# FFN GEMMs of a decoder step in Strassen's scheme: seven block products for eight, by token halves

## The chip, the cores and the metric

The kernel runs on one core of one Trainium2 chip. The metric is device time in microseconds of one launch; lower is better. A profiled execution of the same program gives the trace. All matmuls of interest are float32r: a float32 operand is split exactly into a high and a low float32r part, and one product is made of three matmuls (high by high, high by low, low by high).

## The reference, cut to what matters

One layer of a hybrid decoder on 1088 tokens (1024 prompt tokens and 64 sample tokens) of width 1024: a mixer of sliding-window attention and mLSTM heads, a memory cross-attention, then a SwiGLU FFN with 2816 hidden features, each behind an RMS norm, and a final RMS norm. The change is about the FFN:

```python
def swiglu(xn, w_gate, w_up, w_down):
    g = jnp.einsum('btd,df->btf', xn, w_gate)
    u = jnp.einsum('btd,df->btf', xn, w_up)
    return jnp.einsum('btf,fd->btd', jax.nn.silu(g) * u, w_down)
...
yp = yp + swiglu(rmsnorm(yp, g_ffn[l]), w_gate[l], w_up[l], w_down[l])
y_prompt = rmsnorm(yp, g_final)
```

All outputs, attention caches and mLSTM states among them, are unchanged by the change.

## The kernel before, in words

Activations lie feature-major: eight tiles of 128 features by 1088 tokens. A GEMM takes a weight tile of 128 by 128 as the stationary operand and streams tokens, in three chunks of 384, 384 and 320 columns (`CH`); `mm3` (L133 of the code before) issues the three matmuls of a split product and `gemm_chunk` sums them over the contraction tiles in one PSUM bank. `load_w` (L111) brings a weight tile by one DMA on SP's queue into `wraw`, ScalarE copies it to the high part `whi` (L102) and VectorE subtracts to the low part `wlo` (L103); each of the three has two buffers.

The stages follow one another: the input projection (x arrives, tile by tile, on SP's queue; token-major products `tok_gemm` for v, gates and mv; feature-major products for mq and mk), gates, memory keys, mLSTM in eight blocks of 128 tokens, attention with the output projection as filler, cross-attention by chunks, its output projection `co` with the operands of the FFN's norm (`nx.add` splits y times the norm weights into `nhi` and `nlo`; the norm's factor is applied to the product), and the FFN. In an mLSTM block, GpSimd makes the decay argument (`bc`, L503) and the weighted queries (`wb`, L586); the block's products wait for them.

The FFN runs over 22 hidden tiles in groups of two or four. For each tile: gate product (three chunks of 24 matmuls), the norm's factor on VectorE (L1002), Silu on ScalarE (L1004), the factor again on GpSimd (L1005), the up product, their product `h` (L1008) and its split into `hhi`, `hlo`. After each group the down product of the group is added to y in SBUF (L1018). The last group goes by token chunks of 416, 416 and 256 (`CHE`) with the final norm and the output behind it (L1025, L1032, L1043). FFN weights are read once.

The code is written in a framework that plans the order itself: it records the instructions with their dependences, simulates the engines with costs, and gives each engine the ready instruction that stands first in the code. So an instruction without inputs can stand on its engine far ahead of its place in the code. Each engine then executes in that fixed order, and a waiting instruction holds all behind it on its engine. On-chip buffers come from pools; an instruction that writes a reused buffer waits for its last readers.

Of the kernel before, what the change touches and what calls it, by code (L numbers as in the profile page):

```python
# [9 lines left out]
F32 = mybir.dt.float32  # L10
# [13 lines left out]
CHE = [(0, 416), (416, 832), (832, 1088)]   # where the last one ends the kernel  # L24
FT = 22                     # feature tiles of the FFN
GROUPS = [(0, 2), (2, 6), (6, 10), (10, 14), (14, 18), (18, 22)]
# [3 lines left out]
# columns of the vectors packed by the host  # L30
# [3 lines left out]
# columns of the constants  # L34
C_ID, C_ONE, C_CAUS, C_CAUSS, C_BM, C_M0, C_M1 = 0, 128, 256, 384, 448, 456, 712
C_N = 968
# columns of the constants for the gates
# [5 lines left out]
def tile_hymba_step(  # L43
    ctx: ExitStack,
    tc: tile.TileContext,
    xT, memT, win_f, win_a, win_b, wout, wcq, wck, wcv, wco, wg, wu, wd,
# [6 lines left out]
    cp = ctx.enter_context(tc.tile_pool(name="cp", bufs=1))  # L53
    wp = ctx.enter_context(tc.tile_pool(name="wp", bufs=2))
    sl = ctx.enter_context(tc.tile_pool(name="sl", bufs=1))
    tp = ctx.enter_context(tc.tile_pool(name="tp", bufs=10))
    sm = ctx.enter_context(tc.tile_pool(name="sm", bufs=4))
    dr = ctx.enter_context(tc.tile_pool(name="dr", bufs=1, space=bass.MemoryType.DRAM))
    ps = ctx.enter_context(tc.tile_pool(name="ps", bufs=1, space=bass.MemoryType.PSUM))

    BUFS = {"x": 16, "q": 4, "m": 4, "c": 9, "r": 2}

    def slot(tag, shape, dt=F32, name="slot"):
        return sl.tile([P] + shape, dt, tag=tag, name=name, bufs=BUFS[tag])

# [18 lines left out]
    def mm(out, lhsT, rhs, start=True, stop=True):  # L84
        return TE.matmul(out, lhsT, rhs, start=start, stop=stop)  # L85

# [1 line left out]
    c = cp.tile([P, C_N], F32, name="c")  # L88
    vv = cp.tile([P, V_N], F32, name="vv")
    nc.sync.dma_start(vv, vec)  # L90
    ident = c[:, C_ID:C_ID + P]
    ones = c[:, C_ONE:C_ONE + P]
    epsb = cp.tile([P, 1], F32, name="epsb")
# [29 lines left out]
    def load_ahead(srcs):  # L123
        """The weights in the order of their use, each loaded one step ahead of it."""
        todo, ahead = iter(srcs), []

        def step():
            for src, eng in todo:
                ahead.append(load_w(src, 8, eng=eng))
                break  # L130

        def next_w():
            step()  # L133
            return ahead.pop(0)

        step()
        return next_w

    def mm3(out, ahi, alo, bhi, blo, start, stop):
        mm(out, ahi, bhi, start, False)  # L140
        mm(out, ahi, blo, False, False)
        return mm(out, alo, bhi, False, stop)
# [14 lines left out]
    # ================= stage 1: x, split; sums of squares =================  # L157
    nc.scalar.preload_act_table_set("natural_log_exp_and_others")
    xs, xr = [], []
    for k in range(NK):  # L160
        xr.append(slot("cm"[k % 2], [T], name="xraw"))
        nc.sync.dma_start(xr[k], xT[k])
        hi, lo = slot("x", [T], F32R, name="xhi"), slot("x", [T], F32R, name="xlo")
# [16 lines left out]
    # the first two tiles run along with the arrival of x  # L180
# [24 lines left out]
    # token-major rstd  # L205
# [54 lines left out]
    for b in range(NB + 1):  # L260
        acc, m = tok_gemm(wb, b, 384)
# [94 lines left out]
    # rows (block, head) of prompt; rows (head) of sample  # L356
# [40 lines left out]
    # the weight of the state before the block, as rows  # L397
# [33 lines left out]
    # the upper half of the partitions holds the odd heads  # L431
# [10 lines left out]
    for i, (wi_, pre) in ((1, (2, 0.125)), (2, (3, None)), (3, (4, None))):  # L442
# [3 lines left out]
        for c0, c1 in CH:  # L446
            acc = gemm_chunk(w, xs, c0, c1)
# [4 lines left out]
    # M4: mq pair 0, mq pair 1, mk pair 0, mk pair 1; later the head outputs  # L452
# [4 lines left out]
    # the heads' norm weights with the half of sigmoid(x) = (1 + tanh(x / 2)) / 2  # L457
# [5 lines left out]
    def mlstm_ps():  # L463
        """PSUM for num | den of the heads: the row tiles of odd and even heads go to different banks."""
# [3 lines left out]
    def mlstm_w(src, m):  # L468
        """The weight of the state, by head pair, on the partitions of the heads."""
# [6 lines left out]
    def mlstm_head_out(nb, blk, m, c0, junk):  # L476
        """num | den of the heads in PSUM -> normalised heads, transposed into M4."""
# [22 lines left out]
    def mlstm_S(blk, m, c0, bc, caus):  # L500
        """S^T[s, t] of the four heads, weighted."""
# [73 lines left out]
    for blk in range(NB):  # L575
        if blk == 4:
            mlstm_sample()
# [39 lines left out]
    def softmax_pieces(pieces, mx, nbias, es=None):  # L617
        """P = exp(0.125 s + bias) / (sum + es) in place for the (row, piece) scores."""
# [121 lines left out]
    y = []  # L740

    def load_y():
        for k in range(NK):
            t = slot("mx"[k // 4], [T], name="y")
# [3 lines left out]
    class Next:  # L748
        """Operands of the GEMM behind a norm: (y * g) split; rstd goes on its output."""
# [86 lines left out]
    # weights of this stage in the order of their use  # L836
# [31 lines left out]
    def cross_unit(pair, f):  # L868
        """Two blocks of prompt tokens, one pair of heads."""
# [110 lines left out]
    nx = Next(V_FFN, tags="xxxxxxqq")  # L980
    for ci, (c0, c1) in enumerate(CH):
        for d in range(NK):
            co(d, c0, c1)
            nx.add(d, c0, c1, V if d > 3 else G)
            if ci and d == 1:
                nx.finish([CH[ci - 1]])

# [1 line left out]
    fin = Next(V_FIN, parts=False)  # L989
    for gi, (f0, f1) in enumerate(GROUPS):  # L990
        hs = []
        for f in range(f0, f1):
            wg_, wu_ = load_w(wg[f], NK), load_w(wu[f], NK)
            hi, lo = slot("c", [T], F32R, name="hhi"), slot("c", [T], F32R, name="hlo")
            for c0, c1 in CH:
                n = c1 - c0
                ga = gemm_chunk(wg_, nx.xs, c0, c1)
                if f + c0 == 0:
                    nx.finish([CH[-1]])
                    fr = nx.rstd  # L1000
                t = tmp([384], name="gate")[:, :n]
                V.tensor_tensor(t, ga, fr[:, c0:c1], ALU.mult)  # L1002
                with tc.issue_after(nx.done.ins) if f < 2 else nullcontext():
                    A.activation(t, t, AF.Silu)  # L1004
                G.tensor_tensor(t, t, fr[:, c0:c1], ALU.mult)  # L1005
                ua = gemm_chunk(wu_, nx.xs, c0, c1)
                h = tmp([384], name="h")[:, :n]
                V.tensor_tensor(h, ua, t, ALU.mult)  # L1008
                split(hi[:, c0:c1], lo[:, c0:c1], h)
            hs.append((hi, lo))  # L1010
        nf = f1 - f0
        if gi < len(GROUPS) - 1:
            for d in range(NK):
                if d % 2 == 0:
                    w = load_w([wd[d + i, :, f0:f1, :] for i in range(2)], 2 * nf)
                for c0, c1 in CH:
                    acc = gemm_chunk(w, hs, c0, c1, (d % 2) * nf)
                    V.tensor_tensor(y[d][:, c0:c1], y[d][:, c0:c1], acc, ALU.add)  # L1018
    ws = [load_w([wd[2 * i + z, :, f0:f1, :] for z in range(2)], 2 * nf, tag="x" if i > 1 else None)
          for i in range(4)]  # L1020
    tc.keep_in_program_order(nc.scalar.preload_act_table_set("natural_log_exp_and_others"))

    def out(d, c0, c1):
        t = tmp([448], name="yo")[:, :c1 - c0]
        V.scalar_tensor_tensor(t, y[d][:, c0:c1], gcol(V_FIN, d), fin.rstd[:, c0:c1], ALU.mult, ALU.mult)  # L1025
        nc.sync.dma_start(o_y[d, :, c0:c1], t)

    for ci, (c0, c1) in enumerate(CHE):
        end = ci == len(CHE) - 1
        for d in range(NK):  # L1030
            acc = gemm_chunk(ws[d // 2], hs, c0, c1, (d % 2) * nf)
            V.tensor_tensor(y[d][:, c0:c1], y[d][:, c0:c1], acc, ALU.add)  # L1032
            fin.add(d, c0, c1, V if end and d > 4 else G, end and d == NK - 1)
            if end:
                A.activation(y[d][:, c0:c1], y[d][:, c0:c1], AF.Copy, scale=gcol(V_FIN, d))
            if ci:
                out(d, *CHE[ci - 1])
        fin.finish([(c0, c1)])
    c0, c1 = CHE[-1]
# [136 lines left out]
```

## Time and profile before

| what | value |
|---|---|
| time, median of 3 runs | 1384.12 us (1383.92 to 1391.01) |
| span of the profiled execution, first to last instruction | 1380.3 us |
| own time of the profiled execution | not given; the median is 3.8 us above the span |
| TensorE busy | 1343.5 us, 97% of the span |
| VectorE, ScalarE, GpSimd busy | 622.2, 444.6, 190.3 us |
| moved by DMA | 88.26 MB |

The page is read from the busy table to the slices and then to the chain of waits; the stage that changes is then taken out of the trace by windows. Matmuls are pipelined, so the duration of one (over 300 ns) is no rate: the distance from one start to the next is.

### The profile page before, as it was taken

To read this page: it belongs to the slowest core of one execution; us is meant where nothing else is said; L and a number is where in the kernel's file an instruction comes from. 1 tells how busy PE (TensorE), PEld (TensorE's weight loads), DVE (VectorE), ACT (ScalarE), POOL (GpSimd) and SP (SyncE) were. 2 spreads that over 40 slices of the span, in tenths; PEclk is the share of its full clock that TensorE was granted. 3 is DMA by queue.
4 is the path that set the end of the run, shared out by engine and by line. 5 is a ranking of instruction groups with operands and counts; after the bars stand their busy time and mean duration, and the time that the engine had idled before them with its cause. 6 is when DMAs were issued, how large, how long until landed. Compare 5 with 4: busy or idle time off the path is not lost.

```text
span 1380.3 us, 20544 instructions
## 1 busy us (share of the span) xinstructions
PE 1343.5 (97%) x8352; PEld 1266.2 (92%) x8352; DVE 622.2 (45%) x1373; ACT 444.6 (32%) x1024; POOL 190.3 (14%) x167
## 2 busy tenths in 40 slices
PE   7999999999999898999999999999999999999997
PEld 6999988887888786799999999999999999999997
DVE  7224345467766778835323332332233232423245
ACT  4322332447754666721221011201121121112133
POOL 3000110100003551110111011101110011001123
PEclk9999999999999999999999999999999999999999
DMA  5122413110311224102111111111112120111113
GB/s 228 40 74 62 146 56 121 38 47 16 131 46 57 97 92 163 52 16 62 47 31 62 46 47 31 51 42 46 47 32 61 31 62 31 62 32 50 43 37 124
DMA packets 38807, 88.26 MB, mean 64 GB/s; under 512 B 6593, under 2 KB 14209, under 8 KB 38713
## 3 DMA queue, kind: packets, MB, share of 16 engines
q1 hardware_dynamic: 38713, 86.95, 19.6%
q8 instruction: 66, 1.08, 0.3%
q14 instruction: 28, 0.23, 0.1%
HBM read 79.54 MB, written 7.38 MB: 63 GB/s over the span
## 4 chain that ended last, share of the span: by engine, by line
PE 58%; DVE 3%; ACT 1%; issue 0%; DMA 0%; POOL 0%; DVEq 0%; ACTq 0%; POOLq 0%
PE mm L85 57%; DVE nlo L109 1%; PE o L85 0%; DVE y L955 0%; PE pt L85 0%; DVE nb L866 0%; DVE wlo L103 0%; DMA ck<-cm_k 0%; PE sc L85 0%; ACT sp L887 0%; ACT sq L773 0%; DVE qhl L103 0%; DVE ss L777 0%; DVE yo L1043 0%; PE pt L897 0%
## 5 line engine op out<-in xcount | busy, mean ns | idle before, releaser
L85 PE MATMUL mm<-nhi,wlo 128*128 128x384 f32 (+1 forms) x1056 | 344.4, 326 | 0.0
L85 PE MATMUL mm<-nlo,whi 128*128 128x384 f32 (+1 forms) x1056 | 344.1, 326 | 0.0
L85 PE MATMUL mm<-nhi,whi 128*128 128x384 f32 (+1 forms) x1056 | 344.0, 326 | 0.0
L102 ACT ACTIVATE whi<-wraw 128x1024 fp32r<-128x1024 f32 (+1 forms) x105 | 109.4, 1042 | 345.9 <-PE mm L85 295.1
L85 PEld LDWEIGHTS mm<-nhi,whi 128*128 128x128 f32 x1056 | 198.2, 188 | 0.1
L85 PEld LDWEIGHTS mm<-nhi,wlo 128*128 128x128 f32 x1056 | 198.2, 188 | 0.1
L85 PEld LDWEIGHTS mm<-nlo,whi 128*128 128x128 f32 x1056 | 198.2, 188 | 0.0
L1005 POOL TENSOR_TENSOR gate<-gate,rstd 128x384 f32<-128x384 f32 (+1 forms) x66 | 78.3, 1187 | 656.3 <-ACT gate L1004 656.3
L85 PE MATMUL mm<-hlo,whi 128*128 128x384 f32 (+3 forms) x480 | 157.1, 327 | 0.0
L85 PE MATMUL mm<-hhi,whi 128*128 128x384 f32 (+3 forms) x480 | 156.9, 327 | 0.0
L85 PE MATMUL mm<-hhi,wlo 128*128 128x384 f32 (+3 forms) x480 | 156.9, 327 | 0.0
L103 DVE TENSOR_TENSOR wlo<-wraw,whi 128x1024 fp32r<-128x1024 f32 (+1 forms) x93 | 112.1, 1205 | 45.6 <-ACT whi L102 41.9
L1008 DVE TENSOR_TENSOR h<-mm,gate 128x384 f32<-128x384 f32 (+1 forms) x66 | 35.4, 536 | 193.9 <-PE mm L85 189.0
L1018 DVE TENSOR_TENSOR y<-y,mm 128x384 f32<-128x384 f32 (+1 forms) x120 | 63.6, 531 | 118.6 <-PE mm L85 118.6
L85 PE MATMUL mm<-xhi,whi 128*128 128x384 f32 (+1 forms) x288 | 98.6, 342 | 0.0
L85 PE MATMUL mm<-xlo,whi 128*128 128x384 f32 (+1 forms) x288 | 98.1, 341 | 0.0
L85 PE MATMUL mm<-xhi,wlo 128*128 128x384 f32 (+1 forms) x288 | 97.3, 338 | 0.0
L1002 DVE TENSOR_TENSOR gate<-mm,rstd 128x384 f32<-128x384 f32 (+1 forms) x66 | 35.4, 536 | 123.5 <-PE mm L85 123.5
L85 PEld LDWEIGHTS mm<-hlo,whi 128*128 128x128 f32 x480 | 90.1, 188 | 0.4 <-issue 0.3
L85 PEld LDWEIGHTS mm<-hhi,whi 128*128 128x128 f32 x480 | 90.2, 188 | 0.2 <-issue 0.2
L85 PEld LDWEIGHTS mm<-hhi,wlo 128*128 128x128 f32 x480 | 90.2, 188 | 0.2 <-issue 0.2
L102 ACT ACTIVATE hhi<-h 128x384 fp32r<-128x384 f32 (+1 forms) x66 | 33.2, 503 | 158.7 <-DVE h L1008 158.6
(343 smaller groups left out, 2169.6 us busy)
## 6 DMA issues: line engine op xcount, KB each, us to landing
wraw<-wg SPq DMA_DIRECT2D x22, 512.0 KB
wraw<-wu SPq DMA_DIRECT2D x22, 512.0 KB
wraw<-wd SPq DMA_DIRECT2D x40, 256.0 KB
wraw<-wout SPq DMA_DIRECT2D x32, 256.0 KB
wraw<-win_f SPq DMA_DIRECT2D x13, 512.0 KB
xraw<-xT SPq DMA_DIRECT2D x8, 544.0 KB
y<-xT SPq DMA_DIRECT2D x8, 544.0 KB
o_y<-yo SPq DMA_DIRECT2D x16, 208.0 KB
```

The source lines that it names most:

```text
L85: return TE.matmul(out, lhsT, rhs, start=start, stop=stop)
L102: A.activation(hi, src, AF.Copy)
L103: (eng or V).tensor_tensor(lo, src, hi.bitcast(F32), ALU.subtract)
L109: V.scalar_tensor_tensor(lo, src, scale, hi.bitcast(F32), ALU.mult, ALU.subtract)
L1002: V.tensor_tensor(t, ga, fr[:, c0:c1], ALU.mult)
L1005: G.tensor_tensor(t, t, fr[:, c0:c1], ALU.mult)
L1008: V.tensor_tensor(h, ua, t, ALU.mult)
L1018: V.tensor_tensor(y[d][:, c0:c1], y[d][:, c0:c1], acc, ALU.add)
```

## The change

The FFN's two GEMM kinds are computed by Strassen's scheme in Winograd's variant on 2 by 2 blocks. For gate and up, a block of the weights is half of the contraction (four tiles of 128) by one hidden tile of a pair; a block of the activations is half of the contraction by 272 tokens. For down, a block is one hidden tile of a pair by four output tiles, against 272 tokens of h. The 1088 tokens are processed in two halves of 544 (`z`), each as two blocks of 272; so the FFN weights are now read and split twice.

- **Sums of weight blocks** (`make_sums`): four sums per weight matrix are made in device memory. For each, a DMA on ScalarE's queue copies one block to `sgu` or `sdn`, and an accumulating DMA on GpSimd's queue adds the other. 24 copies and 24 additions, of 4, 4 and 3 pairs each; gate and up sums are 2 MB (1.5 MB for three pairs), down sums half that. Each `next(presum)` issues one copy and the addition for the copy before; there are nine in the token-major loop for mv, nine in the mq and mk chunks, and the rest in the mLSTM blocks.
- **Activation sums** (`parts_of`): from four blocks, N1, T3 on GpSimd, N2, T4 on VectorE, then the split of seven blocks in two groups on ScalarE and VectorE. For x, `ffn_x` first applies the norm's weights and factor; the norm's factors on products are gone.
- **gate_up(pair)**: 7 weight tiles of 128 by 1024 (each two blocks of 512), 14 block products of 12 matmuls with 272 columns, partial results kept by ScalarE copies or added by VectorE from PSUM; Silu and the product; then `parts_of` for h.
- **down(group)**: for two pairs (the last time three), 7 block products over four output tiles, 12 matmuls each per pair, and 28 VectorE additions of PSUM to y.
- **Order**: gate_up of pair 0, then twice gate_up and one down, five times; all for the first 544 tokens, then again for the second.
- **Buffers**: the pools of the earlier stages are closed (`mix.close()`) and the FFN's pools take their place, with weights in 3 raw and 3 split buffers. `co` goes by four chunks of 272 and no longer makes the norm's operands. The final norm of the first half runs beside the second half.

```diff
+    def make_sums():
+        parts = [sums_of(a, b, gu) for gu in (True, False) for a, b in ((0, 4), (4, 8), (8, 11))]
+        last = None
+        for i in range(4):
+            for part in parts:
+                dst, src, plus = part[i]
+                A.dma_start(dst, src)
+                if last:
+                    G.dma_start(last[0], last[1], accum_op=ALU.add)
+                last = dst, plus
+                yield
+        G.dma_start(last[0], last[1], accum_op=ALU.add)
+        yield
...
     for b in range(NB + 1):
+        next(presum)
         acc, m = tok_gemm(wb, b, 384)
...
+    for ci, (c0, c1) in enumerate(CX):
+        ss = tmp([HC], name="ss")
         for d in range(NK):
             co(d, c0, c1)
-            nx.add(d, c0, c1, V if d > 3 else G)
...
+        rstd_of(rf[:, c0:c1], ss)
+    mix.close()
...
+    def parts_of(out, S):
+        G.tensor_tensor(S[:, N1], S[:, B11], S[:, B12], ALU.subtract)
+        G.tensor_tensor(S[:, T3], S[:, B22], S[:, B12], ALU.subtract)
+        A.activation(out[:, 0, 4:7], S[:, 4:7], AF.Copy)
+        V.tensor_tensor(out[:, 1, 4:7], S[:, 4:7], out[:, 0, 4:7].bitcast(F32), ALU.subtract)
+        V.scalar_tensor_tensor(S[:, N2], S[:, N1], -1.0, S[:, B22], ALU.mult, ALU.subtract)
+        V.scalar_tensor_tensor(S[:, T4], S[:, N2], -1.0, S[:, B21], ALU.mult, ALU.subtract)
+        A.activation(out[:, 0, 0:4], S[:, 0:4], AF.Copy)
+        V.tensor_tensor(out[:, 1, 0:4], S[:, 0:4], out[:, 0, 0:4].bitcast(F32), ALU.subtract)
...
+    def prep():
+        for srcs in todo:
+            raw = fp.tile([P, 2, 512], F32, tag="wr", name="wr", bufs=3)
...
+            w = fp.tile([P, 2, 2, 512], F32R, tag="wo", name="wo", bufs=3)
+            A.activation(w[:, 0, :i], raw[:, :i], AF.Copy)
+            V.tensor_tensor(w[:, 1, :i], raw[:, :i], w[:, 0, :i].bitcast(F32), ALU.subtract)
...
+        def prod(b, w, o, i, start, stop):
+            for j in range(4):
+                last = mm3(b, w[:, 0, o, j * P:j * P + P], w[:, 1, o, j * P:j * P + P],
+                           xo[j][:, 0, i], xo[j][:, 1, i], start and j == 0, stop and j == 3, True)
...
+        for z in range(2):
+            w = next_w()
+            b1[z], b2[z] = bank(3 * z), bank(3 * z + 1)
+            prod(b1[z], w, 0, B11, True, True)
+            p1 = keep(b1[z])
+            prod(b2[z], w, 1, B21, True, True)
+            V.tensor_tensor(dst[z](0), b2[z], p1, ALU.add)
+            act(z, 0)
```

## Rows read from the trace of the kernel before

**Rows 1.** The page: busy time and share; the slices of clock and DMA; chain by line.
```profile
PE 1343.5 (97%) x8352; PEld 1266.2 (92%) x8352; DVE 622.2 (45%) x1373; ACT 444.6 (32%) x1024; POOL 190.3 (14%) x167
...
PEclk9999999999999999999999999999999999999999
...
PE mm L85 57%; DVE nlo L109 1%; PE o L85 0%; DVE y L955 0%; PE pt L85 0%; DVE nb L866 0%; DVE wlo L103 0%; DMA ck<-cm_k 0%; PE sc L85 0%; ACT sp L887 0%; ACT sq L773 0%; DVE qhl L103 0%; DVE ss L777 0%; DVE yo L1043 0%; PE pt L897 0%
```

**Rows 2.** Windows: us, busy (instructions) of each engine, granted clock, DMA share, GB/s.
```profile
70.00:583.60 513.60, 496.73 (x3213) 426.46 (x3212) 309.21 (x876) 255.99 (x729) 81.29 (x69) 0.99 0.25 80
...
583.60:1371.20 787.60, 786.02 (x4759) 783.74 (x4758) 272.63 (x437) 156.17 (x247) 98.15 (x86) 1.00 0.15 46
```

**Rows 3.** Waits of TensorE in the FFN, 583 to 1372: us, times, longest.
```profile
PE pt L85 <- POOL ss L777: 1.4, 2, 0.7
```

**Rows 4.** TensorE's starts in streams of equal matmuls: start us, duration us, engine, operation.
```profile
49.95 0.28 PE L85 MATMUL mm<-wtlo,xhi 128*128 128x264 f32 x1
...
67.27 0.28 PE L85 MATMUL mm<-wthi,xhi 128*64 128x264 f32 x1
...
1296.71 0.34 PE L85 MATMUL mm<-nhi,whi 128*128 128x384 f32 x1
...
1312.67 0.33 PE L85 MATMUL mm<-nhi,wlo 128*128 128x384 f32 x1
1312.85 0.31 PE L85 MATMUL mm<-nhi,whi 128*128 128x320 f32 x1
...
1319.73 0.31 PE L85 MATMUL mm<-nhi,wlo 128*128 128x320 f32 x1
...
1362.38 0.28 PE L85 MATMUL mm<-hhi,whi 128*128 128x256 f32 x1
...
1365.02 0.28 PE L85 MATMUL mm<-hlo,whi 128*128 128x256 f32 x1
```

**Rows 5.** Groups by form on VectorE, ScalarE, GpSimd: count, busy us, mean ns, idle before.
```profile
L103 DVE TENSOR_TENSOR wlo<-wraw,whi 128x1024 fp32r<-128x1024 f32 x89 | 109.3, 1228 | 45.4 <-ACT whi L102 41.9 <-issue 3.0 <-DMA bc<-Md 0.5
...
L1032 DVE TENSOR_TENSOR y<-y,mm 128x256 f32<-128x256 f32 x8 | 3.4, 420 | 4.3 <-PE mm L85 4.2
...
L955 DVE TENSOR_TENSOR y<-y,mm 128x320 f32<-128x320 f32 x8 | 3.8, 478 | 0.0
...
L102 ACT ACTIVATE whi<-wraw 128x1024 fp32r<-128x1024 f32 x101 | 106.9, 1059 | 331.2 <-PE mm L85 280.4 <-issue 48.9 <-DMA wraw<-wout 1.1
...
L773 ACT ACTIVATE sq<-y 128x256 f32<-128x256 f32 x7 | 2.9, 418 | 3.2 <-DVE y L1032 3.2
...
L777 POOL TENSOR_TENSOR ss<-ss,sq 128x256 f32<-128x256 f32 x4 | 3.4, 856 | 4.8 <-ACT sq L773 4.8
```

**Rows 6.** Windows of 3 us while x arrives, columns as in rows 2.
```profile
12.00:15.00 3.00, 2.46 (x10) 2.00 (x8) 3.00 (x2) 3.00 (x4) 2.92 (x2) 1.00 1.03 424
...
18.00:21.00 3.00, 2.72 (x17) 2.51 (x16) 3.00 (x2) 0.57 (x2) 3.00 (x5) 1.00 1.02 408
```

**Rows 7.** All engines' first instructions, then SP's queue: start us, duration, instruction.
```profile
1.14 0.27 DVE L461 MEMSET CT<- 128x258 f32 x1
...
13.70 0.33 SPq L273 DMA_DIRECT2D memraw<-memT  x1
```

**Rows 8.** GpSimd's instructions in time, 60 to 620 us.
```profile
154.12 1.30 POOL L503 TENSOR_TENSOR bc<-c,bc 128x512 f32<-128x512 f32 x1 [132.62 <-DMA bc<-Md]
166.11 0.88 POOL L586 TENSOR_TENSOR wb<-mqk,wb 128x128 f32<-128x128 f32 x2 [10.69 <-DMA wb<-Wd]
```

**Rows 9.** The tail, all engines, from the last FFN matmul on.
```profile
1370.90 0.28 PE L85 MATMUL mm<-hhi,wlos 128*128 128x256 f32 x1
...
1371.22 0.42 DVE L1032 TENSOR_TENSOR y<-y,mm 128x256 f32<-128x256 f32 x1
...
1373.83 2.77 DVE L1043 TENSOR_TENSOR yo<-y,rstd 128x256 f32<-128x256 f32 x8 [1.63 <-ACT rstd L155]
```

More of the change, by code (lines that the diff above doesn't have):

```diff
@@ L23 @@
 CH = [(0, 384), (384, 768), (768, 1088)]
-CHE = [(0, 416), (416, 832), (832, 1088)]
 FT = 22
-GROUPS = [(0, 2), (2, 6), (6, 10), (10, 14), (14, 18), (18, 22)]
+NP2 = FT // 2
+HC = 272
+SET = 2 * HC
+CX = [(i * HC, i * HC + HC) for i in range(4)]
 EPS = 1e-6
@@ L575, in tile_hymba_step @@
     for blk in range(NB):
+        next(presum, None)
         if blk == 4:
@@ L989, in tile_hymba_step @@
[L989 to L1038, printed above, removed]
@@ new lines, in tile_hymba_step, with bank @@
+        rstd_of(rf[:, c0:c1], ss)
+    mix.close()
+    N1, N2, T3, T4, B21, B22, B11, B12 = range(8)
+    fp = ctx.enter_context(tc.tile_pool(name="fp", bufs=1, reuse_waits="tile"))
+    fps = ctx.enter_context(tc.tile_pool(name="fps", bufs=1, space=bass.MemoryType.PSUM, reuse_waits="tile"))
+    def bank(i):
+        return fps.tile([P, 512], F32, tag=f"b{i}", name="b")[:, :HC]
+    def parts_of(out, S):
[7 more added lines that the diff above has]
+        V.tensor_tensor(out[:, 1, 0:4], S[:, 0:4], out[:, 0, 0:4].bitcast(F32), ALU.subtract)
@@ new lines, in blocks, with gu_tiles, dn_tiles @@
+    def blocks(name):
+        return fp.tile([P, 8, HC], F32, tag="hs", name=name, bufs=2)
+    def gu_tiles(p):
+        for src, i in ((wgu, 0), (wgu, 2), (sgu, 0), (sgu, 2), (sgu, 4), (sgu, 6), (wgu, 4)):
+            yield [src[p, :, i:i + 2, :]]
+    def dn_tiles(ps_):
+        for src, i in ((wdn, 0), (sdn, 0), (sdn, 2)):
+            for p in ps_:
+                yield [src[p, :, i:i + 2, :]]
+        for i in range(0, len(ps_), 2):
+            yield [wdn[p, :, 2:3, :] for p in ps_[i:i + 2]]
@@ new lines, in next_w, with ffn_x @@
+    def next_w():
+        prep()
+        return ahead.pop(0)
+    prep()
+    def ffn_x(z):
+        xo = []
+        for j in range(4):
+            S = blocks("xs")
+            for i, d in ((B11, j), (B21, j + 4)):
+                V.scalar_tensor_tensor(S[:, i:i + 2].rearrange("p a c -> p (a c)"), y[d][:, z * SET:z * SET + SET],
+                                       gcol(V_FFN, d), rf[:, z * SET:z * SET + SET], ALU.mult, ALU.mult)
+            t = fp.tile([P, 2, 7, HC], F32R, tag="xo", name="xo", bufs=4)
+            parts_of(t, S)
+            xo.append(t)
+        return xo
@@ new lines, in tile_hymba_step @@
+    sg = slot("r", [4, HC], name="sg")
+    for z in range(2):
+        xo = ffn_x(z)
+        ho, used = [], 0
+        for i, (kind, a) in enumerate(plan):
+            if kind == "gu":
+                gate_up(xo, ho)
+            elif z == 1 and i == len(plan) - 1:
+                tc.keep_in_program_order(nc.scalar.preload_act_table_set("natural_log_exp_and_others"))
+                fin = Final(1)
+                down(ho[a[0]:a[-1] + 1], z, fin.add)
+            else:
+                down(ho[a[0]:a[-1] + 1], z)
+            if z == 1 and i == 0:
+                fin = Final(0)
+                for cc in range(2):
+                    for d in range(NK):
+                        fin.add(d, cc)
```

226 lines of the change are left out of this document (190 added, 36 removed).

## The prediction, made before the result was known

> **What bounds the kernel now.** I read the page's busy table first: TensorE is busy for 97% of the span, VectorE for 45%, ScalarE for 32%, and the chain of waits runs for 57% of the span through matmuls of one helper line, at full granted clock in every slice [rows 1]. Then the stage that changes, by windows: the FFN lasts from 583.6 to 1371.2 us, 787.6 us, and holds 4759 matmuls, of which 4752 are its own (3168 for gate and up, 1584 for down) [rows 2]. Its waits are the third view: TensorE waited 1.4 us in it for GpSimd, and for no weights [rows 3]. So the FFN is a pure stream of matmuls, and VectorE's 272.6 us, ScalarE's 156.2 and a DMA share of 0.15 lie hidden under it [rows 2]. Here fewer streamed columns are worth their full time as long as the other engines keep up.
>
> **TensorE's part.** A duration is no rate, so I take distances between starts [rows 4]. 384 columns: 92 steps in 15.96 us, 0.1735 each. 320: 47 steps in 6.88, 0.1464. 264: 143 steps in 17.32, 0.1211. 256: 22 steps in 2.64, 0.1200. 1584 triples of 384, 384 and 320 give 1584 x 0.4934 = 781.5 us, close to the 787.6 measured, so the rates are the right ones. After: a pair takes 14 block products of 12 matmuls for gate and up, 168, and 84 for down; 252 x 11 pairs x 2 halves = 5544 matmuls of 272 columns. No row has 272. Interpolated from 264 and 320 it is 0.1247, from 256 and 320 it is 0.1266; I take the middle, 0.1257: 697 us, with ends at 691 and 702. Streamed columns fall by an eighth, from 1584 x 1088 to 5544 x 272, but the time falls by 11%, since each matmul also costs some 11 to 13 ns beyond its columns and there are 17% more of them.
>
> Here a rule of the Trainium skill (TensorE: Matmul & The Clock Gate, Back-to-back issue gap) can be weighed: at the full clock a matmul should follow the last after its columns at 2.4 GHz plus about 2.5 ns. For 264 columns that is 112.5 ns, where the rows show 121.1; for 272 it would be 115.8 and the FFN an estimated 642 us. The trace disagrees with the rule for these float32r streams, and it is a rival below.
>
> **Can the other engines feed it?** Each weight tile of two blocks serves 24 matmuls, 3.0 us of TensorE, and costs ScalarE 1.06 us and VectorE 1.23 us [rows 5]. A gate_up has 7 such tiles, 21.1 us of TensorE. VectorE: 7 x 1.23, ten operations on 272 columns at about 0.44 (256 take 0.42, 320 take 0.48), and in parts_of a subtraction of 816 and one of 1088 columns and two sums, about 3.2: 16 us, plus up to 1.7 where GpSimd's two subtractions (0.86 each by the 256 row) share its way to memory. ScalarE: 7 x 1.06, ten of 272 at 0.43 and 2.0 for the split: 14 us. A down on two pairs has 7 tiles and 28 additions: VectorE 8.6 + 12.3 = 20.9 against 21.1, and with three pairs about 25 against 31.7. So VectorE goes from 35% to some 85% of the FFN and in the downs is nearly level, by durations; back-to-back operations overlap by some hundredths, so the true load is below that. The products are ordered so that a PSUM bank is reused only after another product of at least 1.5 us, and the next weight tile is prepared a tile ahead. SP must bring 512 KB per 3.0 us, 174 GB/s, where loads ran at 408 to 424 GB/s at full share [rows 6]. I charge 5 us for stalls inside, between 0 and 20. Were the cover gone, each microsecond that VectorE lacks in a down is paid ten times (five downs, two halves).
>
> **Seams of the FFN.** Before, the norm's operands were split along with `co`, and the first FFN matmul followed it without a gap. Now `ffn_x` for the first half is four times two operations on 544 columns (about 0.7 each) and a parts_of of about 3.2: 18 us of VectorE. At least 9 us of it (norm and first split group of four tiles) precede the first product. It can run beside the last two chunks of `co`, 12 us of TensorE, if its buffers lie where earlier stages are already done; the pools of those stages have just been closed, and what overlaps an operand of `co` waits for its end, weights included (a load and a split, some 5 us). I take 8 us, between 0 and 18. At the change of halves the same 18 us of VectorE stand beside the last down (25 of 31.7 taken), and a part of it comes late: 6 us, between 1 and 12. The final norm of the first half (16 squares, 14 additions, 16 products, two table switches) falls into gate_up's slack of 5 to 7 us and spreads over the next ones: nothing taken. Tail: from the last FFN matmul to the span's end it is 9.4 us [rows 9]; after, the last four tiles need one more addition on the chain and slightly wider operations: +1.2.
>
> **The early stretch.** The sums move 34.6 MB by copies (23.1 for gate and up, 11.5 for down) and 34.6 MB by additions, beside 80 GB/s over 513.6 us at a share of 0.25 [rows 2]. No row has a transfer between two places in device memory. If each byte counts once at 415 GB/s, both take 167 us of all queues; if a copy counts twice (read and write) and an addition three times, 417 us. Available between the first idle time and 583.6 us are about 580 - 128 (0.25 x 513.6) - 20 (x at a full share until 21 us [rows 6]) = 430. So the sums are ready in time in either case, at the upper end barely. The copies have no inputs, and rows show such instructions far ahead of their place: the memset of line 461 at 1.1 us and the load of line 273 at 13.7 [rows 7]. So ScalarE's queue may issue many copies while x arrives, when the transfers already run at a share of 1.0 until 21 us [rows 6]. Shared evenly, x comes up to 20 us later. If they keep their place, they share with the mixer's weight loads, which need a quarter of the rate and are prefetched. Issuing itself is short for SP (0.33 us for 128 rows [rows 7]); for a copy of 1024 rows on ScalarE there is no row, and 24 of them at 0.3 to 2.6 us (eightfold) are 8 to 63 us spread over a stretch where ScalarE is half busy. All together I take +18 us, between 0 and 40.
>
> The Trainium skill bears on this (DMA: Bandwidth & Descriptors, Latency and other measured facts): copies from HBM to HBM ran at 207 to 214 GB/s per direction when the row pitch was harmless. By that the copies alone take an estimated 165 us, the case that counts a copy twice; no run here shows it yet.
>
> **The sum.** FFN: 697 + 8 + 6 + 5 = 716 against 787.6, -71.6; tail +1.2; early +18: -52. Span 1380.3 - 52 = 1328. The profile gives no time but its span; the median of the runs is 3.8 us above it, and with that the time is **1332 us**.
>
> **Rivals.**
> *A, GpSimd is held by the additions.* An addition waits for its copy, and on GpSimd everything behind waits too. In the trace the first mLSTM operation of GpSimd (L503) starts at 154.1 us, and each of the eight blocks needs one [rows 8]. If the planner's order puts most additions before it, it starts only when their copies have landed. With copies and additions counted twice each, 333 us of queue time and some 40 for other loads, the last would be at about 375; with half of them ahead of L503, mLSTM starts near 265, 110 us late, and TensorE's fixed order waits with it. For it: nothing hides mLSTM's chain once TensorE has come to it. Against it: GpSimd is idle until 154, so by the lower bound (167 + 40 us) most is over by then. It decides from a delay of about 70 us on. Price: 1332 - 18 + 110 = 1424, slower.
> *B, weight preparation becomes the pace.* Per half, 77 tiles for gate_up and 39 for down, 232 in all, each a handover from DMA to ScalarE to VectorE to TensorE. With 0.25 us lost at each, 58 us in place of 5: 1385, no change. For it: VectorE level with TensorE in the downs. Against it: three buffers, and 2.3 us of work per 3.0.
> *C, the skill's gap rule holds:* 642 for 697, 1277. The 264 row speaks against it.
> That the change doesn't do what it says is unlikely: the count of products is fixed in the code.
>
> **How the numbers follow.** Forecast 0.66, with its own range 1296 (691 us of matmuls, 4 of early cost, 3 of seams and stalls) to 1372 (40 early, and 18 more in seams and stalls of the 31 that their upper ends allow, as these need not fall together); A 0.20; B 0.11; C 0.03. A measurement of this kernel can tell 0.5% (7 us) from no change. Faster: forecast 0.66, C 0.03, 0.03 of B and 0.02 of A: 0.74. Same: 0.05, from B. Slower: the rest of A and of B, 0.21. The range goes from 1296 to 1420: below lie some 0.04, above about half of A and a little more.
>
> **What would show it.** 5544 matmuls of 272 columns, 0.1247 to 0.1266 us apart; few waits of TensorE for `wo`; a gap of about 8 us between `co` and the first product and a smaller one in the middle; copies on ScalarE's queue before 100 us; L503's successor near 154 us plus at most 20. Wrong would make it: GpSimd's first mLSTM operation after 225 us (A), waits of TensorE for VectorE's weight splits adding to more than 40 us (B), or a distance of matmuls outside 0.120 to 0.130 us.

## The result, and the profile after

The changed kernel takes 1546.07 us (median of 4, 1543.41 to 1549.97) against 1384.24 of the kernel before on the same chip: a ratio of 1.117 (95% interval 1.114 to 1.120), slower. The forecast was 1332. Its profiled execution has a span of 1548.2 us, 167.9 above that of before.

Four lines of the page after, beside [rows 1]: the busy table, the granted clock by slices of 38.7 us, the DMA share, and the two new queues with packets, megabytes and share of sixteen engines (q10 carries ScalarE's copies, q0 GpSimd's additions).

```profile
PE 1293.1 (84%) x9194; PEld 1204.5 (78%) x9194; DVE 935.2 (60%) x1854; ACT 679.7 (44%) x1330; POOL 201.5 (13%) x170
...
PEclk9655666999999899999988999999999999999998
DMA  9999999924231022124214555655655655555553
...
q0 software_dynamic: 17280, 34.60, 12.4%
q10 hardware_dynamic: 17280, 34.60, 6.8%
```

TensorE has less to do than before, as meant, but stands idle for most of the first seven slices, where the DMA share is full and the granted clock falls to 0.5. Where the 168 us are is read from marks that both traces have: the first mLSTM operation of GpSimd [rows 8], the first and the last FFN product.

| stretch | before | after | difference |
|---|---|---|---|
| start to GpSimd's first `bc` | 154.1 | 359.8 | +205.7 |
| to the first FFN product | 429.5 | 444.2 | +14.7 |
| first to last FFN product | 787.3 | 729.3 | -58.0 |
| to the end of the span | 9.4 | 14.9 | +5.5 |

So the FFN gained, and nearly all of the loss lies in the early stretch. What TensorE waited for there, from 0 to 380 us (us, times, longest):

```profile
PE pt L90 <- ACT rstd L160: 89.7, 1, 89.7
PE mm L90 <- ACT mvx L297: 73.2, 4, 42.8
```

Both are ScalarE's, the norm's factor and the eviction of mv. What ScalarE did instead is in the view of its copies' line, issues with min, median and max ns, first and last start, and below it who waited behind them:

```profile
L186 ACTq DMA_DIRECT2D sgu<-wgu x12: 592/6684/16977, 0.8 to 209.5; - x12
L186 ACTq DMA_DIRECT2D sdn<-wdn x12: 498/8360/25706, 18.5 to 249.3; - x12
...
  POOL sgu L188: 161.0, 12
  ACT rstd L160: 94.1, 1
```

The planner did put the copies, which have no inputs, ahead of ScalarE's work. An issue that takes half a microsecond at best took 6.7 and 8.4 at the medians and up to 25.7, 187 us summed over the 24, and ScalarE's activations stood behind them. A full DMA share alone does not do it: the issues at 30.9 and 46.4 us still took 0.5 us, at shares of 1.07 and 1.03. By GpSimd's additions, each of which starts when its copy has landed, two earlier copies were unfinished at either; the issue at 56.4 us, with three unfinished, took 6.8 us, and the one at 68.3 us 25.7. The windows show the same stretch (us, busy time and count of each engine, clock, DMA share, GB/s; the count takes in instructions that only reach into a window); the last line is the FFN at its pace:

```profile
75.00:100.00 25.00, 0.00 (x0) 0.00 (x0) 0.00 (x0) 0.00 (x0) 2.34 (x1) 0.50 1.09 254
...
150.00:175.00 25.00, 12.99 (x85) 10.91 (x85) 7.41 (x14) 6.00 (x11) 2.34 (x1) 0.77 1.11 255
...
900.00:950.00 50.00, 50.00 (x403) 50.00 (x402) 36.78 (x52) 27.79 (x41) 4.84 (x4) 1.00 0.56 177
```

From 75 to 150 us no engine computes at all, at a DMA share of 1.08; what counts as GpSimd's busy time there is its issuing of six additions. The distance of matmuls of 272 columns is read from starts, as in [rows 4]:

```profile
903.48 42.12 PE L90 MATMUL b<-xo,wo 128*128 128x272 f32 x336
945.44 6.85 PE L90 MATMUL b<-ho,wo 128*128 128x272 f32 x53
```

That is 336 steps in 41.96 us, 0.1249 us each.

### The profile page after: what moved, and what is told of

The parts are those of the page before. It is cut to its first block, busy times and chain, and to the rows that moved or that the text cites. A ratio compares the mean times of both kernels' runs of the same rounds, so it can differ in the third digit from the quotient of the medians.

```text
span 1548.2 us, 23779 instructions
## 1 busy us (share of the span) xinstructions
PE 1293.1 (84%) x9194; PEld 1204.5 (78%) x9194; DVE 935.2 (60%) x1854; ACT 679.7 (44%) x1330; POOL 201.5 (13%) x170
## 3 DMA queue, kind: packets, MB, share of 16 engines
q0 software_dynamic: 17280, 34.60, 12.4%
q10 hardware_dynamic: 17280, 34.60, 6.8%
## 5 line engine op out<-in xcount | busy, mean ns | idle before, releaser
L90 PE MATMUL b<-xo,wo 128*128 128x272 f32 x3696 | 475.2, 290 | 15.9 <-DVE wo L1103 6.2
L90 PEld LDWEIGHTS b<-xo,wo 128*128 128x128 f32 x3696 | 468.7, 190 | 21.8 <-DVE wo L1103 7.9
L1103 DVE TENSOR_TENSOR wo<-wr,wo 128x1024 fp32r<-128x1024 f32 x232 | 281.0, 1219 | 100.5 <-ACT wo L1102 100.1
L1102 ACT ACTIVATE wo<-wr 128x1024 fp32r<-128x1024 f32 x232 | 243.9, 1053 | 192.3 <-PE b L90 141.9
L90 PE MATMUL b<-ho,wo 128*128 128x272 f32 x1848 | 237.2, 289 | 5.0 <-DVE wo L1103 2.8
L90 PEld LDWEIGHTS b<-ho,wo 128*128 128x128 f32 x1848 | 233.2, 188 | 7.8 <-DVE wo L1103 4.5
L1204 DVE TENSOR_TENSOR y<-y,b 128x272 f32<-128x272 f32 x280 | 103.0, 431 | 4.2 <-PE b L90 4.0
L90 PE MATMUL mm<-chi,wlo 128*128 128x384 f32 (+1 forms) x192 | 63.6, 333 | 1.0 <-POOL wlo L109 1.0
L90 PE MATMUL mm<-chi,whi 128*128 128x384 f32 (+1 forms) x192 | 63.9, 335 | 0.0
L90 PE MATMUL mm<-clo,whi 128*128 128x384 f32 (+1 forms) x192 | 63.1, 329 | 0.0
```

The costliest lines, as they stand in the source:

```text
L90: return TE.matmul(out, lhsT, rhs, start=start, stop=stop, skip_group_check=skip)
L1102: A.activation(w[:, 0, :i], raw[:, :i], AF.Copy)
L1103: V.tensor_tensor(w[:, 1, :i], raw[:, :i], w[:, 0, :i].bitcast(F32), ALU.subtract)
L1204: V.tensor_tensor(y[d][:, c0:c0 + HC], y[d][:, c0:c0 + HC], src[dp], op)
```

## The experiments

Theories: **T1**, ScalarE is held while it issues copies into full queues; **RA**, GpSimd is held by additions that wait for their copies (rival A of the prediction); **R1**, the traffic itself delays loads, whoever issues. All kernels have the changed kernel's products. Ratios are to runs of the kernel before taken beside each kernel; `bc` are first and last start of GpSimd's eight mLSTM additions, FFN the first product.

| kernel | median us | ratio (95%) | bc | FFN from |
|---|---|---|---|---|
| changed kernel | 1546.1 | 1.117 (1.114 to 1.120) | 359.8 to 474.1 | 804.0 |
| e1 no sums | 1343.1 | 0.968 (0.966 to 0.971) | 155.2 to 268.2 | 597.7 |
| e2 copies only | 1401.5 | 1.009 (1.007 to 1.011) | 215.0 to 326.9 | 655.6 |
| e3 copies from GpSimd | 1505.5 | 1.084 (1.081 to 1.087) | 315.1 to 433.8 | 762.6 |
| e4 copies pinned and spread | 1432.9 | 1.033 (1.030 to 1.036) | 167.4 to 329.6 | 686.8 |
| e5 additions pinned too | 1399.1 | 1.011 (1.007 to 1.015) | 161.7 to 303.4 | 650.8 |
| e6 pinned copies only | 1356.7 | 0.980 (0.975 to 0.985) | 155.7 to 277.8 | 610.9 |
| e7 early copies, late additions | 1460.6 | 1.055 (1.050 to 1.060) | 254.4 to 373.5 | 714.1 |
| e8 none in mLSTM, a third in the FFN | 1416.5 | 1.019 (1.013 to 1.025) | 165.2 to 279.7 | 634.3 |
| e9 additions as plain copies | 1378.6 | 0.994 (0.991 to 0.997) | 156.1 to 285.3 | 631.8 |
| e10 sums in SBUF by GpSimd | 1554.5 | 1.120 (1.116 to 1.124) | 154.6 to 271.4 | 603.8 |
| e11 no sums, x without low parts | 1336.6 | 0.964 (0.961 to 0.967) | 157.0 to 269.8 | 600.7 |

**e1, no sums.**
```diff
-    presum = make_sums()
-    for src, i in ((wgu, 0), (wgu, 2), (sgu, 0), (sgu, 2), (sgu, 4), (sgu, 6), (wgu, 4)):
+    for src, i in ((wgu, 0), (wgu, 2), (wgu, 0), (wgu, 2), (wgu, 4), (wgu, 6), (wgu, 4)):
...
```


> Leaves out the sums of weight blocks: no copies, no additions, the FFN reads plain blocks of the weights in their place, with the same bytes and the same matmuls. The changed kernel starts its first mLSTM block 205.7 us later than the kernel before, and by all three theories that comes from the making of the sums: T1 (ScalarE is held while it issues copies into full queues), R1 (297 us of DMA work keep x and the weights waiting, whoever issues), RA (GpSimd is held by its additions). All three: about 1546 - 206 = 1340 us (1330 to 1350), the first mLSTM addition on GpSimd back at 154 (150 to 160), the first FFN matmul at 590 to 602. If the loss is not from the sums at all, it stays above 1500.

1343.1 us; the mLSTM starts at 155.2. The sums cost 0.148 of the time before, 205 us, and the rest of the change gains 3.2%, 44 us.

**e2, copies only.**
```diff
-                if last:
-                    G.dma_start(last[0], last[1], accum_op=ALU.add)
...
```


> Keeps the 24 copies on ScalarE and leaves out the 24 additions (the sums are then unsummed copies). DMA work of the sums falls from 297 to about 105 us of sixteen engines. RA: GpSimd issues nothing, so the loss goes, 1340 us. R1: the loss shrinks with the work, 206 x 105/297 = 73 us left, about 1413. T1: the queues fill less, but ScalarE's 24 issues are still placed ahead of its activations; each drains 1.4 MB at some 330 GB/s (4.4 us), so ScalarE is held up to 105 us less what it gains from two copies in flight: 1400 to 1450, with the time that ScalarE sits in issues of copies (187 us before) falling to 60 to 110.

1401.5, the low end of T1's range and 12 us below R1's 1413; RA's 1340 is out. The issues shrink with the traffic, to 76 us in all, inside T1's 60 to 110 (min, median, max ns):

```profile
L186 ACTq DMA_DIRECT2D sgu<-wgu x12: 717/4106/7914, 0.8 to 105.6; - x12
L186 ACTq DMA_DIRECT2D sdn<-wdn x12: 542/2322/6670, 33.2 to 118.1; - x12
```

**e3, copies from GpSimd.**
```diff
-                A.dma_start(dst, src)
+                G.dma_start(dst, src)
```


> The same copies and additions, the same bytes, but the copies are issued by GpSimd instead of ScalarE. T1: ScalarE is free, so rstd, the evictions of v and mv and the splits run on time; what is left is contention of x (0 to 20 us) and waits for GpSimd: 1340 to 1390. R1: the traffic is the same, so the loss stays: 1520 to 1560. RA: GpSimd is held even longer, the first mLSTM addition comes when the last addition is issued, 290 or later: 1470 or more, with ScalarE idle and not issuing in that stretch.

1505.5, inside RA's range, 15 below R1's and far from T1's 1340 to 1390. The trace tells RA and R1 apart. From 150 to 200 us TensorE is busy all the time (299 matmuls, clock 1.00) at a DMA share of 1.07; from 250 to 300 it does nothing, at 1.09:

```profile
150.00:200.00 50.00, 50.00 (x299) 47.69 (x298) 16.77 (x58) 10.09 (x22) 9.73 (x7) 1.00 1.07 266
...
250.00:300.00 50.00, 0.00 (x0) 0.00 (x0) 0.00 (x0) 0.00 (x0) 10.61 (x8) 0.50 1.09 241
```

So a full share does not stop TensorE. What does is, in ScalarE's waits and TensorE's from 200 to 330 us:

```profile
ACT bc L547 <- POOL bc L545: 94.1, 1, 94.1
```
```profile
PE mm L90 <- ACT whi L108: 95.6, 2, 90.7
```

GpSimd's first `bc` stands behind its transfers, ScalarE's next step behind that `bc`, a weight split behind it, and TensorE behind that. Moving the issues to the idle engine moved the hold there: RA, in a kernel built for it.

**e4, copies pinned and spread.** Each copy is put behind the ScalarE instruction ahead of it in the code, and the 24 are spread from 75 to 580 us.
```diff
-                A.dma_start(dst, src)
+                tc.keep_in_program_order(A.dma_start(dst, src))
...
+        if u % 2 == 0:
+            next(presum)
...
```


> All 24 copies and additions kept, each copy on ScalarE but put in its order behind the ScalarE instruction ahead of it in the program, and spread: 3 in the last token-major GEMM, 3 with mq and mk, 8 with the mLSTM blocks, 8 with every second unit of the sliding-window attention, 3 in the cross-attention, so one about every 20 us from 75 to 560 us instead of all from the start on. T1: ScalarE finds room in the queues at each issue and loses about 1 us at each, 24 us of a stretch in which it is half busy: 1340 to 1365, faster than the kernel before. R1: 297 us of DMA work over 480 us beside a share of 0.2 to 0.4 of the kernel's own: waits for weights come back in smaller size, 1360 to 1420. RA: a GpSimd addition that waits for its copy holds the mLSTM additions behind it, 8 blocks x 10 to 20 us: 1420 to 1500.

1432.9: ScalarE's hold is gone and RA's range is met.

```profile
L186 ACTq DMA_DIRECT2D sgu<-wgu x12: 559/572/678, 74.3 to 484.8; - x12
L186 ACTq DMA_DIRECT2D sdn<-wdn x12: 497/512/542, 77.4 to 581.8; - x12
```

The same instruction costs 0.5 to 0.7 us where the copies are spread. GpSimd's waits from 150 to 340 us, in the mLSTM, show what is late next:

```profile
POOL sgu L188 <- DMA sgu<-wgu: 55.4, 4, 18.5
...
POOL sdn L188 <- DMA sdn<-wdn: 25.7, 2, 13.4
```

**e5, additions pinned and late; e6, the same without additions; e7, additions late, copies early as in the changed kernel.**
```diff
+            dst, plus = late.pop(0)
+            tc.keep_in_program_order(G.dma_start(dst, plus, accum_op=ALU.add))
...
+                late.append((dst, plus))
+                if len(late) > 2:
+                    add()
...
```


> As the spread copies, with all 48 transfers, but each addition is also put in GpSimd's order, behind the GpSimd instruction ahead of it in the program and two steps (some 30 to 40 us) behind its own copy, so that it finds the copy landed. The spread copies lost 90 us against the kernel without sums (1433 against 1343), with GpSimd 375 us in waits of an addition for its copy and ScalarE no longer held (0.5 us an issue). RA' (each hold of an in-order queue costs, first ScalarE's, then GpSimd's): both holds are gone, 24 issues of 1 to 2.6 us on GpSimd are left: 1345 to 1365, GpSimd's waits for copies under 60 us in all. R1 (traffic): the same bytes over the same stretch, so most of the 90 us stay: 1400 to 1435.

> The spread copies on ScalarE alone; the additions are left out. No engine is held; DMA work of the sums is 105 us instead of 297, spread over 500 us. RA': 24 issues of 0.55 us on ScalarE are all that is left, 1343 to 1350. R1 (traffic): a third of what the spread copies with additions lost, 90 x 105/297 = 32 us: 1375.

> The copies as in the changed kernel (free to be issued by ScalarE as early as the order allows, into full queues), the additions on GpSimd late and in order as in the kernel with pinned additions, but for the first five, which come early. ScalarE is held, GpSimd hardly, all bytes are moved. T1+RA' (two holds, that overlap in the changed kernel): what copies alone lost, 1402, give or take 10 us for issues on GpSimd: 1392 to 1415. R1 (traffic): the early stretch holds only the copies, the rest is spread; 1400 to 1440. If the changed kernel's loss were ScalarE's hold alone, at the issue times seen there (187 us), 1500 or more.

e5 took 1399.1: the additions' early place was worth 2.2%, 31 us (GpSimd waits 11.3 us for copies in the stretch where e4 waits 81), but RA's 1345 to 1365 is missed; R1 just misses too. GpSimd's waits for copies add up to 212.8 us over the whole run, not to under 60 as RA had it; TensorE waits for GpSimd no more than 6.0 us, from 60 to 660 us. e6 took 1356.7, between the two. e7 took 1460.6, above all ranges for T1 and R1: ScalarE was held longer than in e2 (`rstd` kept TensorE 54.6 us there, 36.3 in e2), which I put down to the five additions that still stood early; that was not tested by itself, but the trace bears it out for a part: in e7 ScalarE waits 23.9 us for GpSimd's share of the squares of x (`sq`), which stands behind those additions, and in e2 not at all. The changed kernel has the same wait, in ScalarE's waits from 0 to 380 us:

```profile
ACT sq L214 <- POOL sq L218: 23.3, 3, 10.9
```

So traffic has a price of its own, besides the holds.

**e8, none in the mLSTM stretch.** Sums by pair groups; 6 copies ahead of the mLSTM, 4 in the sliding-window attention, 6 in the cross-attention, 8 smaller ones in the FFN's first half.
```diff
...
-        next(presum, None)
         if blk == 4:
             mlstm_sample()
...
         for i, (kind, a) in enumerate(plan):
+            next(presum, None)
```


> All 48 transfers, in order and apart as in the kernel with pinned additions, but none is issued in the mLSTM stretch: 6 copies before it, 4 in the sliding-window attention, 6 in the cross-attention, and the sums of the last three pairs of hidden blocks (8 copies of 0.75 the size) in the first half of the FFN, whose first use of them is some 230 us into it. With the additions pinned the 56 us above the kernel without sums lay: 6.5 ahead of the mLSTM stretch, 29 in it (first to last addition of a row to bc, 141.6 against 113.0), 12 in the sliding-window attention, some 8 in the cross-attention, none in the FFN. If small transfers on the way through the mLSTM (rows of 64 to 256 KB that each block waits for) behind the big ones are what is left of the cost (theory L): 1343 + 8 + 6 + 12 + 0 to 6 = 1365 to 1375, faster than the kernel before. If each byte of the sums costs wherever it is moved (theory R1), the time stays at 1390 to 1405. If the FFN's weight loads suffer (share 0.54 plus some 0.37 in its first half), 1385 or more, with TensorE waiting for wo.

1416.5: a miss for L, with half of it true, and above R1's range; the third forecast, that the FFN's weight loads suffer (1385 or more), is met. The mLSTM is back at 114.5 us from first to last `bc`, as without sums (113.0); the first product comes 36.6 us after e1's, where L had some 26. But the FFN takes 767.5 us from first to last product instead of 728.5. In ScalarE's waits from 650 to 860 us loads of weights stand, which in e1 come to 3.1 us:

```profile
ACT wo L1116 <- DMA wr<-sgu: 21.7, 8, 7.6
...
ACT wo L1116 <- DMA wr<-wgu: 16.2, 9, 3.1
ACT wo L1116 <- DMA wr<-wdn: 15.5, 4, 8.5
ACT wo L1116 <- DMA wr<-sdn: 13.4, 2, 8.0
```
```profile
700.00:750.00 50.00, 43.62 (x309) 41.94 (x308) 32.65 (x52) 19.48 (x26) 7.94 (x6) 0.93 0.96 249
```

At a share of 0.96, 309 matmuls run where e1 has 398. TensorE's own waits there hardly name `wo` (5.3 us), contrary to what I had written: what stood behind the late split on ScalarE and VectorE is named.

**e9, additions as plain copies** (the edit against e5).
```diff
-            tc.keep_in_program_order(G.dma_start(dst, plus, accum_op=ALU.add))
+            tc.keep_in_program_order(G.dma_start(dst, plus))
```


> The kernel with pinned additions, in which each of GpSimd's 24 transfers writes its source over the copy instead of adding it (the sums are left out): same issues, same order, the same waits for the copies, two thirds of the bytes touched. In the traces of the kernels with additions these took 14.4% of sixteen queues' span (201 us), the copies of the same bytes 7.8% (109 us). If the work of the additions in the queues is what is left of the cost, 1399 falls by about (201 - 109)/201 of what additions cost beyond copies alone (1399 - 1357 = 42): 1399 - 19 = 1380 (1374 to 1386). If it is GpSimd's waits and issues, which stay: 1395 to 1400.

1378.6, as the theory of queue work says (1380). In e5 GpSimd's 34.6 MB took 14.4% of the queues' span, 201 us; here the same bytes take 7.6%, 105 us. But the edit changed more than the work in the queues. The plain transfers go in 8832 packets instead of 17280, and GpSimd's 24 issues take 22.5 us instead of 41.0, against the "same issues" of my expectation. The packets explain little, as ScalarE's copies in 17280 packets take 7.8% as well. The shorter issues remain a rival that no run separates; against it speaks that TensorE waits for GpSimd 5.6 us here, from 60 to 660 us, and 6.0 in e5.

**e10, sums in SBUF by GpSimd.** The attempt at a version that beats both kernels. The weight splits go by tiles of half the size, and the last pair gets a down of its own: 336 additions to y instead of 280.
```diff
...
+        r22, r21 = raw(wgu[p, :, 4:6, :]), raw(wgu[p, :, 6:8, :])
+        r1 = [raw(wgu[p, :, 2 * z:2 * z + 2, :]) for z in range(2)]
+        add(r22, r21, r22)
...
+            add(r21[:, z], r21[:, z], r1[z][:, 0])
+            add(r1[z][:, 0], r1[z][:, 0], r22[:, z])
+            yield r1[z][:, 0]
...
```


> No transfer makes sums any more: the FFN loads the four plain blocks of each pair (and one of them a second time, its place being used), and GpSimd adds them in SBUF in place, in both token halves, ahead of the split; the split goes by tiles of half the size. The computation is whole. By what the runs show, the sums cost through the 297 us of transfers and through the waits that they put in front of in-order queues, not through the products: all of that is gone, and the mixer runs as in the kernel without sums (first FFN product at 598). GpSimd adds, per pair of hidden blocks, 2.4 us (an addition of 128x1024 at 2410 ns, as its wlo takes) and 10 additions of half the size at about 1.3: 15.4 us of the pair's 33, beside 3.2 of its own: 56% busy. VectorE's splits in halves cost some 0.06 us more each, 14 us over the FFN, beside 80% busy. Theory S (the sums' transfers were the cost): 1345 to 1365, faster than the kernel before by 1.5 to 3%. Theory D (VectorE and ScalarE feed the products, and GpSimd at work slows them or hands its sums over too late): the FFN takes 760 to 800 instead of 728.5, 1375 to 1415, with TensorE waiting for wo.

1554.5: the mixer is as in e1, and the FFN takes 932.9 us. Theory D, far beyond its range. Three groups of VectorE in e10 (ns min, median, max), then two of e1's:

```profile
L1108 DVE TENSOR_TENSOR wo<-wr,wo x462: 672/686/2932, 608.7 to 1534.0; 128x512 fp32r<-128x512 f32 x154
...
L1150 DVE SCALAR_TENSOR_TENSOR h<-h,sg x66: 428/1065/2156, 630.0 to 1492.6; 128x272 f32<-128x272 f32 x66
...
L1207 DVE TENSOR_TENSOR y<-y,b x336: 421/425/441, 708.2 to 1541.6; 128x272 f32<-128x272 f32 x168
```
```profile
L1110 DVE SCALAR_TENSOR_TENSOR h<-h,sg x66: 426/443/444, 622.4 to 1291.2; 128x272 f32<-128x272 f32 x66
...
L1171 DVE TENSOR_TENSOR y<-y,b x280: 422/430/441, 681.1 to 1330.7; 128x272 f32<-128x272 f32 x140
```

The same operation on 272 columns with both operands in SBUF goes from a median of 443 ns to 1065, while the one with an operand in PSUM stays at 425. The median of the splits `wo`, which also have two operands in SBUF, hides the effect, so I take the instructions one by one. Of the 66 `h`, 23 run beside no GpSimd instruction, and all take at most 444 ns; the 43 others have a median of 1070. Of the 462 splits, 283 run beside none, at 672 to 695 ns; the 179 others have a median of 1644. The 108 additions to y that run beside GpSimd stay at 424. So GpSimd at work slows only the kind with two operands in SBUF. The slowed splits alone are some 132 us of VectorE, which is busy for 839 of 933 us of this FFN and for 588 of 729 in e1; smaller tiles and more additions account for some 60 of the difference. The Trainium skill states this (SBUF — State Buffer, Who interferes with whom): a VectorE instruction with two SBUF inputs contends with a GpSimd instruction that reads SBUF. The trace agrees; I had not weighed the rule against e10's design.

**e11, no sums, and x without low parts.**
```diff
-        V.tensor_tensor(out[:, 1, 4:7], S[:, 4:7], out[:, 0, 4:7].bitcast(F32), ALU.subtract)
+        low and V.tensor_tensor(out[:, 1, 4:7], S[:, 4:7], out[:, 0, 4:7].bitcast(F32), ALU.subtract)
...
-                           xo[j][:, 0, i], xo[j][:, 1, i], start and j == 0, stop and j == 3, True)
+                           xo[j][:, 0, i], xo[j][:, 0, i], start and j == 0, stop and j == 3, True)
```


> The kernel without sums, in which VectorE also does not make the low parts of the seven combinations of x (the products read the high part in their place: same matmuls, low part left out). At the start of the FFN (590 to 620 us of that kernel) TensorE begins 71 matmuls where its pace would be 242: 21 us lost; at the change of halves (930 to 1020) about 100 matmuls are missing, 12 us. Theory X (VectorE's making of x sets both seams; its low parts are 4 x 1.0 and 4 x 1.6 us = 10.3 us for each half): 1343 - 10 - 6 to 10 = 1323 to 1330. Theory N (the norm's chain from the last sum of squares to rstd and then the weights set the start, other work of VectorE the change): within 4 us of 1343.

1336.6, between the theories, and the intervals of e1 and e11 overlap. In the traces the FFN shortens from 728.5 to 721.5 us, and from 610 to 620 us 71 matmuls run instead of 38. So the low parts of x are a part of the seams, some 4 to 7 us (the spans differ by 4.2 us, the FFN's by 7.0). The chain of the changed kernel shows most of the rest of the first seam: from 799.8 to 822.7 us, 19.4 of 22.9 us of it are VectorE's, 16.6 for making x and its low parts and 2.8 for weight splits. In the window below VectorE is busy all the time, and the granted clock is 0.50, TensorE's lower level; what that costs beside VectorE no run separates. The change of halves stays open.

```profile
810.00:816.00 6.00, 3.99 (x16) 3.67 (x17) 6.00 (x7) 1.99 (x2) 2.51 (x2) 0.50 0.25 72
```

**What the runs add up to.** Steps by ratios, in us of 1384: copies, pinned and spread, with their issues on ScalarE (e1 to e6), 16; as many bytes again behind them, with GpSimd's issues (e6 to e9), 19; their addition instead of a copy (e9 to e5), 24; copies put ahead, and with them the first five additions (e5 to e7), 61; the other additions put ahead as well (e7 to the changed kernel), 85. Together 205. That the last step works through ScalarE too is read from its issues (187 us in all against 92 in e7, medians 6.7 and 8.4 us against 4.0 and 2.0) and from TensorE's waits from 0 to 380 us, 163 us for `rstd` and `mvx` against 65 in e7 and 0.9 for GpSimd; no run separates it further. The order of these steps is a choice: copies alone, put ahead (e6 to e2), cost 41.

No version tried that makes the sums beats the kernel before. e5, the best of them with the whole computation, loses by 1.1%: in this order the transfers, even pinned and spread, cost more (59 us, e1 to e5) than the rest of the change gains (44).

## Why the prediction was wrong

- **The early stretch: the failing step.** I wrote that "ScalarE's queue may issue many copies while x arrives" and priced the delay of x (20 us) and the issuing ("24 of them at 0.3 to 2.6 us ... spread over a stretch where ScalarE is half busy"): +18, between 0 and 40. Measured +205.7 to the first `bc`. The order was foreseen; what was missing is that an issue behind several unfinished copies lasts until some of them have landed (up to 25.7 us), and that everything behind it on ScalarE waits. I took the duration of an issue from [rows 7], where the queues had room, for a stretch that I had just filled. The transfers' work itself was inside my bounds: 105 us for the copies and 192 for the additions (6.8% and 12.4% of 1548.2), 297 against 167 to 417. But I put it at nothing beside x ("they share with the mixer's weight loads, which need a quarter of the rate and are prefetched"), and with the transfers pinned and spread it still cost 59 us (e1 to e5).
- **Rival A** had the right kind (an in-order queue held by a transfer) mostly on the wrong engine. It is real where ScalarE is free: e3 shows it whole, e4 against e5 for 31 us. In the changed kernel a small piece of it delays ScalarE, 23.3 us for `sq`. But GpSimd had its additions issued by 288 us and its `bc` came 71 us later, with the work that ScalarE had delayed. My sign that would have told A, `bc` after 225 us, told nothing of who held it.
- **Rival B**, weight preparation as the pace, did not come true: TensorE waited 12.7 us in all for `wo` in the FFN, and a middle stretch runs at 397 to 403 matmuls per 50 us.
- **Rival C** is refuted: 0.1249 us for 272 columns, not 0.1158. The Trainium skill (TensorE: Matmul & The Clock Gate, Back-to-back issue gap) gives the formula behind 0.1158 for the isolated gap of matmuls, and says that in a stream of weight loads and matmuls both set the distance. I had applied it to such a stream.
- **The FFN's products**: 697 us forecast; at 0.1249 they are 692. Right, and inside the interpolation's ends (0.1247 to 0.1266).
- **The seams**: too small. From the last start of the cross-attention's query split (`qhl`) to the first product it is 37.0 us where it was 21.8, and from 804 to 828 us 79 matmuls begin for 192 at full pace (14.1 us): 29 us where I took 8, between 0 and 18. At the change of halves some 112 are missing (14 us; 6, between 1 and 12). Inside, some 9 us (5, between 0 and 20). The tail is +5.5, not +1.2. Its chain, after (start us, us, what):

```profile
1532.51 0.82 DVE y L1204 x2
1533.32 3.31 DVE yo L1267 x8
1536.63 0.35 DVE ss L1254
```

  VectorE writes eight output tiles of the chunk that ended first before it sums the squares of the last one; [rows 9] has no such step on the path.
- **Sum without the early stretch**: I forecast -70; e1's span is 39.1 below that of before. So the gain of the FFN was overstated by 31 us, and even without any cost of sums the time would have been 1343 and not 1314.

## What to carry to other kernels

A transfer that is "in the background" still has to be issued by someone: price its issue at the number of transfers that the change itself leaves waiting, and ask what stands behind it on the issuing engine. Instructions without inputs need an anchor in the order; pinning copies and additions to spread places gave back 146 of 205 us without a byte less. What then remained went with the transfers' work: in the mLSTM, which was back to its length once none ran there, and in the FFN, where weight loads came late beside them (e8). Which of the mLSTM's own transfers were late was not shown.

## What the runs showed of the hardware that I had not expected

- A DMA issue on ScalarE took 0.5 us with two earlier copies unfinished, even at DMA shares of 1.03 and 1.07, and 5.0 to 25.7 us soon after with more of them unfinished; it held the engine.
- Moving 34.6 MB between places in device memory took 105 to 109 us of sixteen engines' time, 318 to 330 GB/s (e2 from 50 to 75 us, with no engine computing: 319 GB/s at a share of 1.01); adding as many onto others took 192 to 201 us, 1.8 to 1.9 times that, each landing 28 to 42 us after its issue in the changed kernel.
- The Trainium skill's 207 to 214 GB/s (DMA: Bandwidth & Descriptors, Latency and other measured facts), by which I had an estimated 165 us for the copies, did not hold here. The page gives them for other layouts, with rows of 16 KiB that lie 512 KiB or more apart.
- Two of VectorE's operations with two SBUF operands (`h` and the splits `wo`) took more than twice as long when they ran beside an addition of GpSimd's in SBUF (medians 442 against 1070 ns, 684 against 1644); those with an operand in PSUM did not change.
